# A hybrid encoder step on one core: the last chunk of the down projection splits its own late weight blocks, and its norms, copies and splits stand in another order

## The chip, the cores and the metric

The kernel runs on one core of a Trainium2 chip. The metric is the device time of one execution in microseconds (us). Three runs of the kernel before gave 1445.07, 1445.33 and 1449.37 us; their median is 1445.33 us.

## The reference, cut to what matters

One layer of an encoder works on 1024 prompt rows and 64 sample rows of width 1024, in float32. Three groups of heads mix the rows, a layer norm follows, and then the part that this change touches:

```python
def sq_relu_mlp(x, w_up, w_down):
    h = jnp.square(jax.nn.relu(jnp.einsum('btd,df->btf', x, w_up)))
    return jnp.einsum('btf,fd->btd', h, w_down)
...
        xp = layer_norm(ALPHA * xp + sq_relu_mlp(xp, w_up[l], w_down[l]), ln2_g[l], ln2_b[l])
```

`w_up` is 1024 x 4096 and `w_down` 4096 x 1024. The layer norm takes mean and variance over the 1024 values of a row and then multiplies by `ln2_g` and adds `ln2_b`.

## The kernel before, in words

TensorE (PE) multiplies float32 as three passes over a high and a low part in a rounded format. Every operand is **split** once (line 1182 is ACT's copy to the high part, line 97 the subtraction that makes the low part, on DVE or POOL). The split of h is a helper of its own, `h_split` (lines 1396, 1400, 1401): ACT copies a half to its high part, ACT copies that into a bank of PSUM (tile `st`, banks `o` and `tr` in turn), DVE subtracts.

The stages are: input projection, attention, output projection and first norm (to about 690 us), up projection (PE, line 1242, to about 1060 us), and **down**, from there to the end. h lies in DRAM, already transposed and combined.

**Down** runs over 8 chunks c of 512 rows of `w_down`. A chunk has two steps g = 2c and 2c + 1, each for half of the token tiles, and a step has two chains (class `Down`), one for tiles i and i + 4. A chain is seven products (`DOWN`), a Winograd form of a 2 x 2 block product; a product is 6 matmuls of 128 x 512. Products n = 0, 2, 4, 6 add up in one bank A, n = 1 goes into a bank B that ACT has filled beforehand (`preload`, line 1558), n = 3 and 5 into a bank D. Between two products into the same bank the bank must be read: after n = 0 by ACT (tile `p`, line 1587), after the others by DVE (line 1537, or 1580 where the sum of a row for the norm is taken along). So product n = 2 waits for the read of n = 0, n = 4 for that of n = 2, n = 5 for that of n = 3. Products 0 to 3 use h's first array (loaded into `awa`), 4 to 6 its second (`hr`, split by `h_split(g, 1, x)`).

The weights of chunk c + 1 are made during chunk c, one part q in each step. `wd_load` brings a raw part (512 KB twice) into the one buffer `rd`. Seven blocks are split from it (`wd_split`, k = 0 to 6): k = 0, 1, 2 from the raw blocks, then POOL overwrites them with differences (`wd_sums`, line 1371, four subtractions, called sum 0 to sum 3 here), and k = 3 to 6 are split from those: k = 4 needs sum 0, k = 5 sum 1, k = 3 sum 2, k = 6 sum 3. Sum 1 must also wait until DVE has split raw block 1 for the sample rows (tile `b`, one buffer, so its ACT copy waits for the previous chunk's sample products). The next part can be loaded only when all of this has read `rd`. The product order needs k = 0, 1, 3, 4, 5, 2, 6; k = 1, 2 are also read by `sample` (16 matmuls, lines 1614 and 1616).

**What sets the order.** In the loop over chunks a planner orders the instructions of every engine by its own estimate of time, so that a small edit can move instructions anywhere in the loop. The last chunk (c = 7, steps 14 and 15, four chains) stands in `in_order()`: on each engine its instructions keep the order of the source. `do(k, n)` is product n of chain k with the read of its bank. Between the products stand the layer norm of finished tiles: `neg_mean` (DVE), `squares` (ACT with a running sum, then POOL's `scale`, lines 1638 and 1639), `shift` (POOL), `normalize` (ACT, line 1663), `times` and `plus` (POOL, lines 1667 and 1671, and the store), or for the last tiles `on_dve` (lines 1679 and 1681) with copies of `ln2_g` and `ln2_b` in PSUM that `put_gb` makes (line 1731). ACT, DVE and POOL work their instructions off in order, so a waiting instruction holds back all behind it.

Of the kernel before, what the change touches and what calls it, by code (L numbers as in the profile page):

```python
# [12 lines left out]
F32 = mybir.dt.float32  # L13
# [43 lines left out]
def _build(nc, tc, a, es):  # L57
# [20 lines left out]
    def bcast(row, n=P):  # L78
        return row.broadcast_to([n, row.shape[-1]])
# [1279 lines left out]
    def wd_split(c, q, n, eng):  # L1359
        w = wset[c % 2][q]  # L1360
        b, src = ((0, 0), (1, 2), (2, 3), (5, 3), (3, 0), (4, 1), (6, 2))[n]
        split(w[:, 0, b], w[:, 1, b], raws[c, q][:, src], eng)
# [27 lines left out]
    def h_split(g, which, x, only=None):  # L1390

        for q in range(2):
            t = h_tile(g, which, x)
            o = 3 if which else 4
            raw = hraw[which, q][:, :, x * P:(x + 1) * P]
            nc.scalar.activation(t[:, 0, q], raw, AF.Copy)
            tag = only or ("o", "tr")[n_stage[0] % 2]
            n_stage[0] += 1
            st = ps.tile([P, 4, P], F32, name=f"st{n_stage[0]}", tag=tag, bufs=1)[:, 0:o]
            nc.scalar.activation(st, t[:, 0, q].bitcast(F32), AF.Copy)  # L1400
            nc.vector.tensor_tensor(t[:, 1, q], raw, st, op=ALU.subtract)  # L1401
# [104 lines left out]
    with ExitStack() as p3:  # L1506
# [100 lines left out]
        def sample(c):  # L1607
            for half in range(2):
                z = ps.tile([P, 512], F32, name=f"ds{c}_{half}", tag="s" if c < NC - 1 else ("s", "pt")[half], bufs=2)
                for q in range(2):  # L1610
                    for f in range(2):

                        w = b12[q] if f == 0 and half else wset[c % 2][q][:, :, f + half]
                        nc.tensor.matmul(z, hs[:, q, f].rearrange("p h c -> p (h c)"), w[:, 0],
                                         start=(q == 0 and f == 0), stop=False, skip_group_check=True)
                        nc.tensor.matmul(z[0:TS], hs[:, q, f, 0], w[:, 1], start=False, stop=(q == 1 and f == 1),
                                         skip_group_check=True)
                add(c == 0, acc[NB, half], z)
# [26 lines left out]
        def squares(t):  # L1645
            st = norm(t)

            nc.scalar.activation(awa[:, 0], accf[t], AF.Square, bias=st[:, 12:13], accum_out=st[:, 13:14])
            scale(t, P, 1.0 / D)
# [11 lines left out]
        def normalize(t, n=P, c0=0):  # L1661
            y, st = accf[t][0:n, c0:D], norm(t)[0:n]
            nc.scalar.activation(y, y, AF.Identity, bias=st[:, 15:16], scale=st[:, 14:15])

        def times(t, n=P, c0=0):
            y = accf[t][0:n, c0:D]
            nc.gpsimd.tensor_tensor(y, y, g2[0:n, c0:D], op=ALU.mult)

        def plus(t, n=P, c0=0):
            y = accf[t][0:n, c0:D]  # L1670
            nc.gpsimd.tensor_tensor(y, y, b2[0:n, c0:D], op=ALU.add)
            nc.sync.dma_start(out_rows(t)[:, c0:D], y)
# [11 lines left out]
        for c in range(NC - 1):  # L1684
            for part in range(2):
                g = 2 * c + part
                wd_load(c + 1, part)
                ch = [Down(g, x) for x in range(2)]
                for q in range(2):
                    h_load(g + 1, 0, q)  # L1690
                for n in range(7):
                    for d in ch:
                        d.product(n)
                    for d in ch:
                        d.evac(n)
                    if n < 2:
                        h_split(g, 1, n)
                    if n == 1:
                        for q in range(2):
                            h_load(g + 1, 1, q)  # L1700
                    if n == 3 and part == 0:
                        sample(c)
                        hs_load(c + 1)
                    if n in (2, 4):
                        h_split(g + 1, 0, n // 2 - 1)
                    if n == 1:
                        for k in range(3):
                            wd_split(c + 1, part, k, nc.gpsimd)
                    if n == 3:
                        wd_b12(c + 1, part, nc.vector)  # L1710
                        wd_sums(c + 1, part, nc.gpsimd)
                    if n == 4:
                        for k in range(3, 7):
                            wd_split(c + 1, part, k, nc.vector if k in (4, 5) else nc.gpsimd)


        c = NC - 1
        gb2 = lp.tile([P, 2, D], F32, name="gb2", tag="wr")
        g2, b2 = gb2[:, 0], gb2[:, 1]
        nc.sync.dma_start(g2, bcast(a["ln2_g"]))  # L1720
        nc.sync.dma_start(b2, bcast(a["ln2_b"]))
        fixed = {b: ps.tile([P, 512], F32, name=f"last{b}", tag=tag, bufs=2) for b, tag in (("B", "s"), ("D", "pt"))}
        gbp = []
        ch = [Down(2 * c + k // 2, k % 2, fixed, norm) for k in range(4)]
# [3 lines left out]
        def put_gb():  # L1728
            for q, (src, tag) in enumerate(((g2, "o"), (g2, "tr"), (b2, "s"), (b2, "pt"))):
                gbp.append(ps.tile([P, 512], F32, name=f"gbp{q}", tag=tag, bufs=1 if q < 2 else 2))  # L1730
                nc.scalar.activation(gbp[q], src[:, q % 2 * 512:q % 2 * 512 + 512], AF.Copy)

        def do(k, n):
            ch[k].product(n)
            ch[k].evac(n)
# [8 lines left out]
        with in_order():  # L1744
            ch[0].preload()
            do(0, 0)
            h_split(g, 1, 0)
            do(0, 1)
            sample(c)
            do(0, 2)  # L1750
            h_split(g, 1, 1)
            for q in range(2):
                h_load(g + 1, 1, q)
            do(0, 3)
            fold(0)
            fold(1)
            h_split(g + 1, 0, 0)
            do(0, 4)
            moments(NB, 0, TS)
            moments(NB, 1, TS)  # L1760
            scale(NB, TS)
            shift(NB, TS, -1.0)
            ch[1].preload()
            do(0, 5)
            neg_mean(0)
            do(1, 0)
            h_split(g + 1, 0, 1)
            do(0, 6)
            neg_mean(4)
            normalize(NB, TS)  # L1770
            times(NB, TS)
            squares(0)
            shift(0)
            do(1, 1)
            plus(NB, TS)
            squares(4)
            shift(4)
            normalize(0)
            times(0)
            plus(0)  # L1780
            do(1, 2)
            h_split(g + 1, 1, 0)
            do(1, 3)
            h_split(g + 1, 1, 1)
            ch[2].preload()
            do(1, 4)
            do(1, 5)
            neg_mean(1)
            do(2, 0)
            put_gb()  # L1790
            normalize(4)
            times(4)
            do(1, 6)
            neg_mean(5)
            squares(1)
            shift(1)
            plus(4)
            do(2, 1)
            squares(5)
            normalize(1)  # L1800
            times(1)
            do(2, 2)
            on_dve(5, 0, 0)
            ch[3].preload()
            do(2, 3)
            on_dve(5, 1, 0)
            do(2, 4)
            on_dve(5, 0, 1)
            do(2, 5)
            neg_mean(2)  # L1810
            on_dve(5, 1, 1)
            squares(2)
            shift(2)
            plus(1)
            do(3, 0)
            normalize(2, c0=512)
            do(2, 6)
            neg_mean(6)
            squares(6)
            times(2, c0=512)  # L1820
            plus(2, c0=512)
            do(3, 1)
            on_dve(2, 0, 0)
            on_dve(2, 0, 1)
            do(3, 2)
            on_dve(6, 0, 0)
            do(3, 3)
            on_dve(6, 0, 1)
            do(3, 4)
            on_dve(6, 1, 0)  # L1830
            do(3, 5)
            neg_mean(3)
            squares(3)
            on_dve(6, 1, 1)
            do(3, 6)
            neg_mean(7)
            squares(7)
            for i in range(2):
                for step in range(2):
                    on_dve(3, i, step)  # L1840
            shift(7)
            normalize(7, c0=768)
            times(7, c0=768)
            plus(7, c0=768)
            for c0, c1 in ((0, 512), (512, 768)):
                for step in range(2):
                    on_dve(7, c0 // 512, step, c1)
# [23 lines left out]
```

## Time and profile before

| | |
|---|---|
| time of the profiled execution | 1445.71 us |
| its span, first to last instruction | 1444.0 us |
| instructions | 24224 |
| busy: PE / DVE / ACT / POOL | 93% / 70% / 50% / 42% of the span |
| PE, 1120 to 1249 us (three chunks of down) | busy throughout |
| PE, 1400 to 1425 us | 19.41 of 25 us, granted clock 0.86 |
| PE, 1425 to 1445 us | 8.42 of 20 us |

The rows of a timeline give start, duration, engine, line, operation, output and inputs, a count, and in brackets the time that the engine stood idle before it and what released it. A wait put down to one engine can hide another that had to be waited for as well. Matmuls overlap: back to back, one of 128 x 512 starts every 0.232 us (six in 1.39 us) though its row shows 0.39.

### The profile page before, as it was taken

The numbers are of one execution on the slowest core, as the hardware profiler recorded it, in microseconds if no ns is written. First come the engines' busy times: TensorE is split into PE (matmuls) and PEld (weight loads), VectorE is DVE, ScalarE is ACT, GpSimd is POOL, SyncE is SP. The second block draws the span as 40 slices with busy tenths as digits, with TensorE's granted clock in tenths as the row PEclk, the third lists the DMA queues.
The fourth block names the chain that finished last, engine by engine and source line by source line (L and its number), as shares of the span: only waits on it lengthen the run. The fifth ranks groups of instructions, "written<-read, shape, count | busy, mean of one in ns | idle before, by whom it ended". The sixth has DMA issues, their size and how long they took to land.

```text
span 1444.0 us, 24224 instructions
## 1 busy us (share of the span) xinstructions
PE 1337.6 (93%) x8827; PEld 1212.3 (84%) x8827; DVE 1009.8 (70%) x1802; ACT 720.3 (50%) x1561; POOL 610.6 (42%) x660
## 2 busy tenths in 40 slices
PE   7899999999999988989779999999959999999976
PEld 6899999998988986867779999999947787777755
DVE  3567565767885699786736877776677766777766
ACT  3366565656564674243323323222345666766664
POOL 2222323266564537564222222222245464655565
PEclk9999999999999999999989999999979999999998
DMA  7324232322213435331124434443484424334333
GB/s 212 80 75 111 62 106 72 78 55 65 64 34 83 131 98 154 125 101 42 54 86 163 165 116 160 148 136 129 161 281 163 164 95 150 136 127 150 113 106 117
DMA packets 146207, 168.59 MB, mean 117 GB/s; under 512 B 27036, under 2 KB 112348, under 8 KB 146088
## 3 DMA queue, kind: packets, MB, share of 16 engines
q1 hardware_dynamic: 146088, 167.04, 36.7%
q8 instruction: 70, 1.15, 0.3%
q14 instruction: 49, 0.40, 0.1%
HBM read 109.00 MB, written 51.71 MB: 111 GB/s over the span
## 4 chain that ended last, share of the span: by engine, by line
PE 58%; DVE 12%; POOL 9%; DMA 8%; ACT 6%; issue 6%; SPq 1%; DVEq 0%; POOLq 0%; ACTq 0%
PE zA L1242 9%; PE zD L1242 6%; PE kvfox L337 5%; PE kvsb L337 5%; PE A L1570 4%; PE zB L1242 3%; PE zC L1242 3%; POOL rd L1371 3%; POOL wd L97 3%; PE mx L232 3%; DMA rd<-w_down 2%; PE qfox L478 2%; PE D L1570 2%; PE Sfox L536 2%; PE qsb L478 2%
## 5 line engine op out<-in xcount | busy, mean ns | idle before, releaser
L97 POOL TENSOR_TENSOR wa<-wr,wa 128x512 fp32r<-128x512 f32 x45 | 68.7, 1554 | 230.2 <-ACT wa L1182 230.2
L97 POOL TENSOR_TENSOR wd<-rd,wd 128x512 fp32r<-128x512 f32 x80 | 109.4, 1382 | 87.5 <-ACT wd L1182 82.0
L232 PE MATMUL mx<-xT,oTb 128*128 128x512 f32 (+1 forms) x416 | 106.3, 407 | 3.0 <-ACT oTb L191 2.0
L1182 ACT ACTIVATE wd<-rd 128x512 fp32r<-128x512 f32 x112 | 68.3, 625 | 75.1 <-DMA rd<-w_down 30.7
L1242 PE MATMUL zA<-xo,ws 128*128 128x288 f32 (+1 forms) x720 | 96.7, 289 | 2.5 <-ACT sn L1251 2.5
L1242 PE MATMUL zD<-xo,ws 128*128 128x288 f32 (+1 forms) x720 | 98.3, 291 | 0.0
L1251 ACT ACTIVATE sn<-zA 128x288 f32<-128x288 f32 (+1 forms) x96 | 37.6, 393 | 119.8 <-PE zA L1242 106.4
L232 PEld LDWEIGHTS mx<-xT,oTb 128*128 128x128 f32 (+1 forms) x416 | 77.2, 191 | 22.6 <-ACT oTb L191 3.0
L1242 PEld LDWEIGHTS zA<-xo,ws 128*128 128x128 f32 x720 | 93.4, 189 | 3.0 <-ACT sn L1251 2.9
L1242 PEld LDWEIGHTS zD<-xo,ws 128*128 128x128 f32 x720 | 94.8, 191 | 0.2
L337 PE MATMUL kvfox<-wkvfox,xT 128*128 128x256 f32 (+3 forms) x624 | 91.6, 296 | 3.1 <-DVE fx L440 2.0
L522 POOL TENSOR_TENSOR sgsb<-sgsb,snsb 128x127 f32<-128x127 f32 (+7 forms) x48 | 58.8, 1227 | 78.5 <-DVE snsb L520 67.6
L1371 POOL TENSOR_TENSOR rd<-rd 128x512 f32<-128x512 f32 x56 | 81.1, 1448 | 22.7 <-DVE b L97 20.3
L337 PE MATMUL kvsb<-wkvsb,xT 128*128 128x256 f32 (+1 forms) x624 | 88.2, 287 | 0.0
L337 PEld LDWEIGHTS kvfox<-wkvfox,xT 128*128 128x128 f32 (+1 forms) x624 | 82.8, 196 | 4.7 <-DVE fx L440 2.2
L1570 PE MATMUL A<-wd,wd 128*128 128x512 f32 x312 | 84.9, 401 | 2.0 <-ACT p L1587 0.7
L520 DVE TENSOR_TENSOR_SCAN snsb<-snsb,one 128x128 f32<-128x128 f32 (+7 forms) x48 | 72.1, 1506 | 13.2 <-ACT snsb L519 12.6
L337 PEld LDWEIGHTS kvsb<-wkvsb,xT 128*128 128x128 f32 (+1 forms) x624 | 79.7, 188 | 0.2
L1570 PE MATMUL A<-wd,h4a 128*128 128x512 f32 x240 | 67.1, 402 | 9.9 <-POOL wd L97 4.7
L1570 PEld LDWEIGHTS A<-wd,wd 128*128 128x128 f32 x312 | 58.8, 191 | 19.2 <-DVE acc L1537 2.9
L1570 PEld LDWEIGHTS A<-wd,h4a 128*128 128x128 f32 x240 | 44.8, 190 | 23.6 <-POOL wd L97 6.5
L1401 DVE TENSOR_TENSOR wd<-hr,st 128x384 fp32r<-128x384 f32 x64 | 34.7, 550 | 39.3 <-ACT st L1400 39.2
(511 smaller groups left out, 3745.6 us busy)
## 6 DMA issues: line engine op xcount, KB each, us to landing
rd<-w_down SPq DMA_DIRECT2D x32, 512.0 KB, 4.5
awa<-h_dr SPq DMA_DIRECT2D x32, 512.0 KB, 4.5
wr<-w_up SPq DMA_DIRECT2D x15, 1024.0 KB, 5.5
h_dr<-hh SPq DMA_DIRECT2D x30, 512.0 KB, 3.2
hr<-h_dr SPq DMA_DIRECT2D x32, 384.0 KB, 3.1
h_dr<-hh SPq DMA_DIRECT2D x30, 384.0 KB, 3.2
raw<-w_in SPq DMA_DIRECT2D x44, 256.0 KB, 3.4
xr<-x_prompt SPq DMA_DIRECT2D x8, 512.0 KB, 6.2
```

The lines of the kernel that those rows point to most:

```text
L97: eng.tensor_tensor(out, src, hi.bitcast(F32), op=ALU.subtract)
L232: nc.tensor.matmul(acc[0:m], oT[:, k, hx, 0:m], wo[k // 4][hw][:, k % 4, cs], start=(i == 0), stop=(i == len(seq) - 1))
L337: nc.tensor.matmul(acc[0:n, c0:c0 + n1 - n0], xT[k // 4][:, k % 4, c:c + n], wt[:, k, hw, n0:n1], start=(i == 0), stop=(i == len(seq) - 1))
L478: nc.tensor.matmul(acc[:, 0:w], wq[:, k, hw, :], xT[k // 4][:, k % 4, c:c + w], start=(i == 0), stop=(i == len(seq) - 1))
L520: nc.vector.tensor_tensor_scan(g[:, 0:n][:, ::-1], g[:, 0:n][:, ::-1], one.broadcast_to([P, n]), 1.0, op0=ALU.mult, op1=ALU.bypass)
L522: nc.gpsimd.tensor_tensor(s[:, 0:n - 1], s[:, 0:n - 1], g[:, 1:n], op=ALU.mult)
L1182: nc.scalar.activation(hi, raw, AF.Copy)
L1242: nc.tensor.matmul(z, w[:, hw, k], xop(s, bo, hx)[:, k, :], start=(new and k == 0 and j == 0), stop=(k == 3 and j == 2), skip_group_check= ...
L1251: nc.scalar.activation(sn[:, (0, None, 1, None, 2)[i], 0:n], z, AF.Copy)
L1371: eng.tensor_tensor(r[:, o], r[:, x], r[:, y], op=ALU.subtract)
L1401: nc.vector.tensor_tensor(t[:, 1, q], raw, st, op=ALU.subtract)
L1570: nc.tensor.matmul(z, h[:, hx, q, o], wset[self.c % 2][q][:, hw, wb], start=((n in (0, 3) or n == 1 and self.c == 0) and q == 0 and j == 0 ...
```

## The change

In the loop, the low parts of k = 3 to 6 go to DVE, POOL, DVE, POOL instead of POOL, DVE, DVE, POOL; and in step 13 (the last of the loop, g = 13) these four splits are not issued any more. They stand in the last chunk instead, behind the products n = 0 and n = 1 of its first chain and behind `sample`, with low parts on POOL, DVE, DVE, POOL. The load of `ln2_g` and `ln2_b`, which goes into the same buffer as `rd`, moves behind them. Further on, the second splits of h for the third and fourth chain, the preload of the third chain, `put_gb`, and the norm of tile 4 change places:

```diff
                     if n == 4:
-                        for k in range(3, 7):
-                            wd_split(c + 1, part, k, nc.vector if k in (4, 5) else nc.gpsimd)
+
+                        for k in range(3, 7) if g < NP - 3 else ():
+                            wd_split(c + 1, part, k, (nc.gpsimd, nc.vector)[k % 2])
...
-        gb2 = lp.tile([P, 2, D], F32, name="gb2", tag="wr")
-        g2, b2 = gb2[:, 0], gb2[:, 1]
-        nc.sync.dma_start(g2, bcast(a["ln2_g"]))
-        nc.sync.dma_start(b2, bcast(a["ln2_b"]))
...
             do(0, 0)
+            wd_split(c, 1, 3, nc.gpsimd)
             h_split(g, 1, 0)
             do(0, 1)
+            wd_split(c, 1, 4, nc.vector)
             sample(c)
+            wd_split(c, 1, 5, nc.vector)
+            wd_split(c, 1, 6, nc.gpsimd)
+            gb2 = lp.tile([P, 2, D], F32, name="gb2", tag="wr")
+            g2, b2 = gb2[:, 0], gb2[:, 1]
+            nc.sync.dma_start(g2, bcast(a["ln2_g"]))
+            nc.sync.dma_start(b2, bcast(a["ln2_b"]))
             do(0, 2)
...
             do(1, 2)
-            h_split(g + 1, 1, 0)
+            ch[2].preload()
             do(1, 3)
-            h_split(g + 1, 1, 1)
-            ch[2].preload()
+            normalize(4)
+            times(4)
             do(1, 4)
+            plus(4)
             do(1, 5)
             neg_mean(1)
             do(2, 0)
-            put_gb()
-            normalize(4)
-            times(4)
+            h_split(g + 1, 1, 0)
             do(1, 6)
             neg_mean(5)
             squares(1)
             shift(1)
-            plus(4)
             do(2, 1)
+            h_split(g + 1, 1, 1)
+            put_gb()
             squares(5)
             normalize(1)
             times(1)
...
             on_dve(5, 1, 1)
+            do(3, 0)
             squares(2)
             shift(2)
             plus(1)
-            do(3, 0)
             normalize(2, c0=512)
```

No instruction is added or dropped. Down to the first chunk of down every engine has the same order as before; from there on the planner orders the loop anew.

## The prediction

> **What bounds the kernel now.** I read PE's timeline from 1040 us on, then ACT's, DVE's and POOL's over the last 100 us, then the granted clock in small windows. From 1120 to 1249 us PE is busy throughout, so whatever the planner reorders there can gain nothing; it can only lose. PE waits at the edge to the last chunk and once inside it:
>
> ```profile
> 1373.60 0.50 PE L1570 MATMUL A<-wd,h4a 128*128 128x512 f32 x1 [0.33 <-ACT wd L1182]
> 1374.95 0.73 PE L1570 MATMUL A<-wd,h4a 128*128 128x512 f32 x2 [0.84 <-POOL wd L97]
> 1376.10 0.96 PE L1570 MATMUL A<-wd,wd 128*128 128x512 f32 x3 [0.41 <-DVE acc L1537]
> ...
> 1382.05 1.66 PE L1570 MATMUL lastB<-wd,h4a 128*128 128x512 f32 x6 [1.13 <-ACT lastB L1558]
> ...
> 1407.07 2.92 PE L1570 MATMUL lastD<-wd,wd 128*128 128x512 f32 x6 [4.90 <-DVE acc L1537]
> 1409.79 4.16 PE L1570 MATMUL A<-wd,wd 128*128 128x512 f32 x12
> ```
>
> The first four waits are the edge: part 1 of chunk 7's weights comes late. The fifth is inside chunk 7, and the matmuls behind it are slow: the windows (length, then busy time of PE, PEld, DVE, ACT, POOL, then the clock) show why.
>
> ```profile
> 1402.00:1407.00 5.00, 0.17 (x1) 0.00 (x0) 1.69 (x4) 4.23 (x8) 4.67 (x7) 0.86 0.19 40
> 1407.00:1410.00 3.00, 2.93 (x7) 2.35 (x8) 1.64 (x5) 1.25 (x3) 2.92 (x2) 0.50 0.10 21
> 1410.00:1413.00 3.00, 3.00 (x9) 2.34 (x9) 0.91 (x3) 0.41 (x1) 0.89 (x1) 0.59 0.43 173
> ```
>
> 18 matmuls take 6.72 us from 1407.07 to 1413.79 where 18 x 0.232 would be 4.18: the idle stretch costs 4.9 + 2.5 = 7.4 us.
>
> **The edge.** POOL and ACT tell why part 1 is late:
>
> ```profile
> 1361.80 1.30 POOL L1371 TENSOR_TENSOR rd<-rd 128x512 f32<-128x512 f32 x1 [9.84 <-DVE b L97]
> ...
> 1366.87 2.56 POOL L97 TENSOR_TENSOR wd<-rd,wd 128x512 fp32r<-128x512 f32 x2
> ```
> ```profile
> 1380.88 0.63 ACT L1182 ACTIVATE wd<-rd 128x512 fp32r<-128x512 f32 x1 [3.63 <-POOL rd L1371]
> 1381.42 0.58 ACT L1558 ACTIVATE lastB<-awa 128x512 f32<-128x512 f32 x1
> ```
>
> In step 12 POOL idles 9.84 us until DVE has split `b` (ACT's copy at 1360.32), then does three sums, the sample's two and k = 3, 6; at 1369.43 the buffer is free, the load goes out at 1369.46 and the copy starts at 1372.92. Now, by the new orders:
>
> - k = 4 is POOL's (1.28 us) and lies in the 9.84 us of idleness; one low part, not two, follows the sums. 1.28 us earlier.
> - ACT's copy of `b` stood behind two copies of `hr` and an `st` (1359.07 to 1360.32); now it comes right behind the copies of `awa`. Those wait for loads that waited for DVE's reads of `awa`; DVE no longer has the split of k = 4 (1.16) and a bank read (0.60) ahead of these, of which I count 1.3, as `st` comes at 1351.65. So `b` at 1357.8; `sample` is 6 matmuls earlier in PE's order and done by 1355.9.
> - Sums from 1359.1: 1.30 + 0.89 + 3.01 to 1364.3; ACT's last copy for k = 6 stands behind that of k = 3 and a `p`, so k = 6 ends at 1366.2; DVE's k = 3 (1.5 us beside POOL) by 1365.1. Free 3.2 us earlier, the load's copy at 1369.7.
>
> PE comes to part 1's first matmul at 1371.75, so its three waits for it go. Next late is DVE's low part of `b` (copy 1370.3 to 1370.8, 1.34 us) with three instructions of 0.60 behind it: the read that the next product waits for ends at 1373.9, PE comes at 1373.85. The preload of B (1381.42) stood behind a copy that waited for sum 1; now it stands ahead of it. With no wait left the 30 matmuls from 1371.05 end at 1378.1 and lastB starts there, not at 1382.05: 3.9 us. Behind it the moved splits: k = 3's low part (POOL) ends at 1381.6 and is needed at 1383.3, k = 4 (DVE, behind B's read) at 1383.9 for 1384.7, k = 5 at 1385.7 for 1386.1; their reads of the bank push n = 4 by 0.3 and n = 5 by 0.2, and the copies for `fold` (1390.04 before) come at 1386.85. So what hangs on ACT and DVE in chain 0 is **3.2 us** earlier; POOL's `times(NB)` follows. The load of `ln2_g` moves behind k = 5 (1385.8, before 1386.44); it is needed 10 us later. SP's second `hr` load now waits behind the weights' load; it is read 12 us later. Bounds: 1.3 (only POOL's one instruction counts) and 4.0.
>
> **The tail.** I give it in the old clock and take the 3.2 us off at the end. The wait of 4.90 is this: ACT's `normalize(0)` (1402.68) waits for POOL's `times(NB)` and `scale(0)`; h's splits stand behind it on ACT, DVE's subtraction behind them, and behind that the read of D:
>
> ```profile
> 1402.68 1.24 ACT L1663 ACTIVATE awa<-awa,lstb 128x1024 f32<-128x1024 f32 x1 [1.30 <-POOL lstb L1659]
> 1403.83 0.51 ACT L1396 ACTIVATE wd<-hr 128x384 fp32r<-128x384 f32 x1
> ```
>
> With the splits gone, DVE reads D at once and PE goes on at 1402.1. Now what comes late:
>
> - ACT: `normalize(0)` to 1403.9, preload to 1404.45; `normalize(4)` waits for POOL's `plus(NB)` (1402.60 to 1404.94) and `scale(4)`, `shift(4)` to 1406.11: 1406.15 to 1407.4. Then `p` of chain 2 to 1407.9 (PE is there at 1407.7), two copies and two `st` (0.97 a pair, as at 1403.92 to 1405.82) to 1409.85, `squares(1)` (1.15) to 1411.0, the other four to 1412.95.
> - DVE's subtractions for these end at 1413.5 and stand ahead of the read of A after (2, 2): 1414.15. PE has finished (2, 3) at 1410.8 and starts (2, 4) at 1414.2: **a new wait of 3.4 us**. Before, (2, 4) started at 1417.99.
> - `put_gb` now follows (2.15 us, to 1415.1), then `squares(5)` to 1416.3, which `on_dve(5)` must wait for since it overwrites what is squared; the read of D after (2, 3) stands behind that, 1417.65. (2, 5) starts at 1417.7, having waited 2.1 us; before at 1420.24.
> - POOL: `times(0)`, `plus(0)`, `times(4)`, `plus(4)` (2.37 to 2.40 each) fill it from 1406.1 to 1415.7, `scale(5)` ends at 1417.6; DVE needs it at 1419.0. `normalize(1)` ends at 1417.9, the preload of chain 3 at 1418.4, needed at 1421.9.
> - (3, 0) now precedes `squares(2)` on ACT, so its `p` is ready before (3, 2) and the wait of 0.72 at 1426.83 goes. PE's last product starts at 1428.95 (1432.57 before). DVE is then the bound: its last eight `on_dve` start at 1431.75, not 1435.15. **3.4 us** earlier; behind them nothing changes.
>
> **Sum.** 3.2 + 3.4 = 6.6 us off the profiled execution's 1445.71: **1439.1 us** (the median of the runs, 1445.33, is 0.4 below that execution; against it the gain is 6.2 us or 0.43%).
>
> **The loop.** Over chunks 0 to 6 I count nothing. For step 10 by the new orders: the two preloads of B are done at 1319.65 and 1323.2, PE needs them at 1320.7 and 1323.75; `p` at 1322.0 for 1322.35. Bounds: 1.5 gained (the waits of 1.04 at 1276.02, 0.34 and 0.15 later go) and the price of the third rival.
>
> **Rivals.**
>
> 1. *The clock falls in the new wait.* For: the 4.90 us of idleness above were followed by 0.50. Against: 3.4 us is shorter, and the 2.45 us before 1051.25 left the clock at 1.00 in the window of 1051 to 1054. At half speed (2, 4) takes 2.8 us, which the wait for (2, 5) hides; (2, 5) and part of (3, 0) would lose 2 us: 1441.1. The Trainium skill ("TensorE: Matmul & The Clock Gate", "What's actually happening") says that the clock is halved after at least one idle window of about 3.4 us and that the window runs freely; by it a gap of 3.4 us seldom covers a whole one, and the sum stays. The trace agrees on the half (0.50); where its windows lie it can't show.
> 2. *The wait only moves.* If the copies, `squares(1)` and `put_gb` cost what the old wait did, (2, 4) and (2, 5) start 3.4 us later than I say and the edge alone is left: 1442.5. For: the eight copies stand in front of (2, 4) now. Likewise if the load comes only 1.3 us sooner: 1441.0.
> 3. *The loop gets slower: the case on the other side.* In the loop ACT now has the preloads of B behind the copies for k = 5 and 6 and `p` behind k = 3, all waiting for POOL's sums. My slack is 0.35 to 1.05 us. A sum takes 1.25 to 1.63 us; if three take the upper value more often than I reckon, the preload is late. At 1.0 us in each of 13 parts PE loses 13 us: 1452.1, slower. It decides from 0.5 us a part, where the gain is gone. For: any wait there is a loss, PE having no slack. Against: the waits of this kind in the old loop came to 1.5 us in all.
>
> **How the numbers follow.** About 0.3% (4.3 us) can be told from no change. My forecast, between 1436 and 1441: 54%. The clock or the moved wait, 1441 to 1443: 26%. The loop: 20%, half of it only eating the gain (1443 to 1449), half slower than that. So faster 0.55, within 0.34, slower 0.11. The range goes from 1436.0 (4.0 at the edge, 3.4 in the tail and 1.5 in the loop give 1436.8; 0.8 more should the new waits be shorter) to 1446.5, which leaves out most of the slower loop.
>
> **What would show it.** Right: lastB starts straight behind g = 13's last matmul; the load of part 1 is issued about 3 us before its place now; (1, 5) follows (1, 4) without a wait; the longest wait of PE in chunk 7 is ahead of (2, 4), 3 to 4 us, released by DVE, with the clock at 1.00 behind it; then 2 us ahead of (2, 5). Wrong: waits of PE for ACT's `B` or `p` spread over the loop, a clock of 0.5 behind the new wait, or a last `on_dve` group that starts no earlier relative to PE's last product.

## The result, and the profile after

The changed kernel takes **1438.82 us**, the median of six runs (1437.36 to 1442.09). Beside them the kernel before has 1446.62 us, also of six. The ratio is 0.9948, with a 95% interval of 0.9932 to 0.9964: 5.2 to 9.8 us less. The profiled execution of the changed kernel took 1441.04 us, 4.67 less than that of before.

PE's timeline of the profile after, at the edge and then inside the last chunk (start, duration, operation, count, and in brackets the wait and its releaser):

```profile
1376.57 0.84 PE L1570 MATMUL A<-wd 128*128 128x512 f32 x3
1377.47 1.66 PE L1570 MATMUL lastB<-wd,h4a 128*128 128x512 f32 x6
...
1404.89 1.56 PE L1570 MATMUL lastD<-wd,wd 128*128 128x512 f32 x6
1409.64 2.90 PE L1570 MATMUL A<-wd,wd 128*128 128x512 f32 x6 [3.18 <-DVE acc L1537]
1413.17 2.93 PE L1570 MATMUL lastD<-wd,wd 128*128 128x512 f32 x6 [0.63 <-DVE acc L1537]
1415.89 4.44 PE L1570 MATMUL A<-wd,wd 128*128 128x512 f32 x12
```

The four waits of the edge are gone: lastB starts straight behind the matmuls ahead of it, 4.58 us earlier than before. The wait of 4.90 is gone too, and in its place one of 3.18 stands ahead of (2,4), product 4 of chain 2. The windows of the same execution (length, busy time of PE, PEld, DVE, ACT, POOL, then the clock) show what followed it:

```profile
1406.00:1409.00 3.00, 0.45 (x2) 0.01 (x1) 2.47 (x8) 2.83 (x8) 2.92 (x3) 0.98 0.44 175
1409.00:1412.00 3.00, 2.36 (x6) 1.84 (x6) 0.72 (x2) 2.73 (x5) 2.83 (x3) 0.50 0.00 0
1412.00:1415.00 3.00, 2.37 (x6) 1.49 (x5) 3.00 (x6) 1.73 (x2) 2.31 (x5) 0.50 0.44 178
1415.00:1418.00 3.00, 3.00 (x8) 2.31 (x7) 1.61 (x5) 0.00 (x0) 1.05 (x1) 0.50 0.23 87
1418.00:1421.00 3.00, 3.00 (x12) 2.42 (x11) 0.63 (x2) 1.73 (x3) 0.41 (x2) 0.81 0.23 87
```

The clock is at 0.50 for some 10 us, longer than before (from 1405.6 to 1412.5 there). So the last eight `on_dve` start at 1430.22, 4.93 us earlier than before, hardly more than lastB: in this execution the new tail is worth 0.35 us.

The edge itself, on POOL, ACT and SP's queue of the profile after:

```profile
1356.21 0.77 POOL L97 TENSOR_TENSOR hs<-acc,hs 128x128 fp32r<-128x128 f32 x1 [5.71 <-ACT hs L1182]
1356.94 1.30 POOL L1371 TENSOR_TENSOR rd<-rd 128x512 f32<-128x512 f32 x1
...
1362.69 1.30 POOL L97 TENSOR_TENSOR wd<-rd,wd 128x512 fp32r<-128x512 f32 x1 [1.07 <-ACT wd L1182]
```
```profile
1364.02 0.81 SPq L1357 DMA_DIRECT2D rd<-w_down  x2
```

POOL's idle time of 9.84 ahead of sum 1 is 5.71 now, one low part instead of two follows the sums, and the load of part 1 goes out at 1364.02 instead of 1369.46. On ACT the copies of h are gone from behind `normalize(0)`; a preload follows it at once:

```profile
1398.07 1.25 ACT L1663 ACTIVATE awa<-awa,lstb 128x1024 f32<-128x1024 f32 x1 [1.29 <-POOL lstb L1659]
1399.22 0.58 ACT L1558 ACTIVATE lastB<-acc 128x512 f32<-128x512 f32 x1
```

To see where the time went, I divided each profiled execution at four marks: the four matmuls into A that wait for POOL's low part (1072.44 before), the first matmul `ds<-b` of chunk 0 (1091.13), the first into lastB (1382.05), and the last eight `on_dve` (1435.15). Between the first two lies the **head**, between the next two **loop and edge**, then the **tail**. Loop and edge hold the same 1220 matmuls in all kernels; in most of it one starts every 0.231 us, which makes 281.8 us of work for PE.

| execution | shares in the loop | head starts | head | loop and edge | tail | clock behind the tail's first wait |
|---|---|---|---|---|---|---|
| before | old | 1072.44 | 18.69 | 290.92 | 53.10 | 0.50 |
| e2_tail | old | 1069.87 | 18.59 | 294.78 | 52.57 | 0.50 |
| e4_moved | old | 1065.85 | 19.69 | 295.51 | 52.08 | 0.50 |
| e8_late | old up to step 11 | 1069.62 | 22.34 | 292.02 | 52.66 | 0.50 |
| after | new | 1072.34 | 21.30 | 283.83 | 52.75 | 0.50 |
| after_again | new | 1072.59 | 20.65 | 283.63 | 50.10 | 1.00 |
| e1_edge | new | 1069.44 | 19.86 | 283.64 | 52.94 | 0.50 |
| e3_swap | new | 1069.86 | 19.89 | 284.52 | 52.52 | 0.50 |
| e5_fill | new | 1073.80 | 20.81 | 282.60 | 50.10 | 1.00 |
| e6_early | new | 1073.76 | 20.73 | 282.95 | 48.02 | 1.00 |
| e6_again | new | 1071.87 | 20.78 | 284.98 | 48.04 | 1.00 |
| e7_alt | other alternation | 1070.33 | 19.81 | 283.38 | 53.01 | 0.50 |
| e10_both | other alternation | 1073.13 | 18.81 | 286.27 | 48.03 | 1.00 |
| e9_first | old in step 0, then new | 1075.25 | 18.80 | 284.34 | 48.00 | 1.00 |

Before against after: the head starts 0.10 earlier and takes 2.61 longer, loop and edge take 7.09 less, the tail 0.35 less, and what lies behind it 0.23 more: -4.70, the difference of the spans. The start of the head differs by some 9 us from execution to execution; nothing ahead of it is changed in any kernel. Three heads hold one more wait, for DVE's read L1535 late in the head: e4_moved 1.13, e7_alt 1.26, e8_late 2.53.

### The profile page after: what moved, and what is told of

Same layout as the page of the kernel before. It is cut to its first block, busy times and chain, and to the rows that moved or that the text cites. A ratio compares the mean times of both kernels' runs of the same rounds, so it can differ in the third digit from the quotient of the medians.

```text
span 1439.3 us, 24229 instructions
## 1 busy us (share of the span) xinstructions
PE 1340.2 (93%) x8827; PEld 1217.8 (85%) x8827; DVE 1010.3 (70%) x1802; ACT 720.3 (50%) x1561; POOL 610.5 (42%) x660
## 4 chain that ended last, share of the span: by engine, by line
PE 67%; DVE 9%; DMA 7%; ACT 7%; POOL 4%; issue 4%; SPq 1%; DVEq 0%; ACTq 0%; POOLq 0%
PE zA L1242 9%; PE mx L232 7%; PE zD L1242 6%; PE A L1570 6%; PE kvsb L337 5%; PE kvfox L337 4%; PE zB L1242 3%; PE zC L1242 3%; PE D L1570 3%; PE qsb L478 2%; DMA rd<-w_down 2%; PE qfox L478 2%; POOL wd L97 2%; PE Sfox L536 2%; PE B L1570 1%
## 5 line engine op out<-in xcount | busy, mean ns | idle before, releaser
L1438 ACT ACTIVATE ws<-wr 128x1024 fp32r<-128x1024 f32 x30 | 31.2, 1057 | 58.4 <-DVE wr L1192 58.4
```

The lines of the kernel that those rows point to most:

```text
L1438: nc.scalar.activation(ws[:, 0, q], raw[:, q], AF.Copy)
```

## The experiments

Twelve runs, in three groups of four; those of one group share a chip and the runs of the kernel before (medians 1445.62, 1448.15 and 1448.33 us).

**e1_edge: the loop's and the edge's part of the change, the old tail.** Against the changed kernel:

```diff
             do(1, 2)
-            ch[2].preload()
+            h_split(g + 1, 1, 0)
             do(1, 3)
-            normalize(4)
-            times(4)
+            h_split(g + 1, 1, 1)
+            ch[2].preload()
             do(1, 4)
-            plus(4)
...
```

> The loop's new shares and the late splits inside chunk 7, with the old order from product (1, 2) on. I read two stretches: L, from the second sample group of chunk 0 (b row) to lastB's first start (290.92 us before, 283.83 after), and T, from there to the end of the last on_dve (58.55 before, 58.20 after). Theory: loop and edge are a gain of their own, L as after (283 to 285), T as before (58 to 59, with the wait of 4.9 and the clock of 0.5 behind it), so about 7 us faster than before. Rival (the wait only moves): what is won at the edge is waited for again in chunk 7, T 3 us or more longer, 0 to 4 us faster.

Measured: 1436.70 us (1435.21 to 1441.16), ratio 0.9945 (0.992 to 0.997); loop and edge 283.64, tail 52.94. None of the edge's four waits is left, the wait of 4.9 inside the chunk is back. So loop and edge hold the whole gain that the medians show.

**e2_tail: the kernel before with the new tail alone.** Against before:

```diff
             do(1, 2)
-            h_split(g + 1, 1, 0)
+            ch[2].preload()
             do(1, 3)
-            h_split(g + 1, 1, 1)
-            ch[2].preload()
+            normalize(4)
+            times(4)
             do(1, 4)
+            plus(4)
...
```

> The old loop and the old edge, with the new order from product (1, 2) on. Theory: L as before (290 to 291); the wait of 4.9 goes, a new one of 3.2 ahead of (2, 4) comes, T 55 to 56 if the clock stays at 1.00 behind it, 58 if it falls to 0.5: 3 us faster or the same as before, by the clock. Rival (the tail is the whole gain): 5 us or more faster.

Measured: 1446.60 us (1439.96 to 1451.80), ratio 1.0003 (0.9982 to 1.0024). The wait ahead of (2,4) is 3.20, the clock fell behind it, the tail takes 52.57. No gain that can be measured.

**e3_swap: the other shares in all 14 steps, nothing else.**

```diff
                         for k in range(3, 7):
-                            wd_split(c + 1, part, k, nc.vector if k in (4, 5) else nc.gpsimd)
+                            wd_split(c + 1, part, k, (nc.gpsimd, nc.vector)[k % 2])
```

> Only the shares of the low parts in the loop as after, in all 14 steps; the splits of k = 3 to 6 of the last part stay in step 13, and chunk 7 keeps its old order. Theory: k = 4 lies in POOL's idle time and the load of part 1 goes out 3 to 5 us sooner than before, so the loop and the first three waits of the edge gain, 5 to 6 us, L 285 to 286; lastB still waits for ACT, whose copies for the sums stand ahead of its preload (about 1 us). Rival (the late splits in chunk 7 are the gain): L 289 or more, within 2 us of before.

Measured: 1439.04 us (1434.89 to 1442.28), ratio 0.9951 (0.9935 to 0.9966); loop and edge 284.52, within a microsecond of the whole change. At the edge a single wait of 1.34 for DVE's read is left. This one line makes the measurable gain by itself, though the title names only the last chunk's part of the change.

**e4_moved: only the late splits moved into the last chunk; old shares, old tail.**

```diff
-                        for k in range(3, 7):
+                        for k in range(3, 7) if g < NP - 3 else ():
...
             do(0, 0)
+            wd_split(c, 1, 3, nc.gpsimd)
...
+            wd_split(c, 1, 4, nc.vector)
```

> Only the last part's splits of k = 3 to 6 inside chunk 7; shares in the loop and the order from (1, 2) on as before. Theory: part 1's load is as late as before, the waits of 0.33, 0.84 and 0.41 at the edge stay, only lastB's preload comes sooner: L 289 to 290, 1 to 2 us faster. Rival (late splits are the gain): L 284 to 286, 5 to 7 us faster.

Measured: 1444.79 us (1442.27 to 1449.90), ratio 1.0004 (0.9986 to 1.0021); loop and edge 295.51, above both theories. The wait of 1.13 ahead of lastB is gone, but the three ahead of it stand (0.41, 0.84, 0.41), and the clock fell among them, from 1375.1 to 1378.5. The moved splits alone bring nothing.

**after_again: the changed kernel once more.**

> The changed kernel once more, beside the three others of this call. Theory (the gain is the loop's and the edge's, the tail's is lost to the granted clock): a median of 1437 to 1440 us, from the second sample group of chunk 0 to the first product into lastB 283 to 285 us (283.83 in the first profile), from there to the last eight on_dve 52.5 to 53 us if the clock falls again behind the new wait ahead of (2,4), 49.5 to 50 us if it does not. Rival (the head and the clock differ by chance from execution to execution): the head's products at 0.50 this time only until 1078, as in the profile before, and so a lastB some 2 to 3 us earlier.

Measured: 1437.36 us (1432.22 to 1444.21), ratio 0.9928 (0.9905 to 0.9952). The head was again at half clock up to 1087, and loop and edge took 283.63; but the tail took 50.10 instead of 52.75. Its windows:

```profile
1406.00:1409.00 3.00, 0.00 (x0) 0.00 (x0) 2.43 (x6) 2.83 (x7) 2.92 (x2) 1.00 0.43 175
1409.00:1412.00 3.00, 1.63 (x6) 1.05 (x6) 0.79 (x2) 2.33 (x5) 2.67 (x5) 1.00 0.17 72
1412.00:1415.00 3.00, 2.39 (x10) 1.99 (x11) 3.00 (x6) 1.58 (x2) 2.47 (x3) 1.00 0.25 105
```

The same program with the same wait (3.19) ahead of (2,4), and the clock did not fall. This is the tail as I forecast it: 3.00 us shorter than before's. The difference between the two executions, 2.65 us, is what the half clock costs.

**e5_fill: twelve more matmuls in the new wait.** They go into the bank that (3,0) uses later.

```diff
+        def fill(n):
+            ch[3].open("A")
+            for k in range(n):
+                nc.tensor.matmul(ch[3].bank["A"], h_tile(2 * c + 1, 0, 0)[:, 0, 0, 0], wset[c % 2][0][:, 0, 0],
+                                 start=(k == 0), stop=(k == n - 1), skip_group_check=True)
...
             do(2, 3)
+            fill(12)
```

> The changed kernel with twelve more matmuls of 128 x 512 behind product (2,3), into the bank that product (3,0) overwrites later, so that PE works in the new wait ahead of (2,4); their result is not used. Theory (the wait itself costs little at the end, the half clock behind it costs about 3 us): the wait is gone or under 0.5 us, the clock stays at 1.00 from 1406 to 1425, lastB to the last eight on_dve takes 49.5 to 50.5 us instead of 52.75, and the kernel is 2 to 3.5 us faster than the changed one. Rival (DVE and ACT's order sets the end, not the clock): clock at 1.00, but 52 us and more as before, no faster than the changed kernel.

Measured: 1438.16 us (1436.37 to 1439.21), ratio 0.9931 (0.9914 to 0.9949). The clock stays at 1.00 and the tail takes 50.10, as in after_again to the hundredth: (2,4) starts 32.21 us behind lastB in both, so the fill neither delays it nor brings it sooner. The gain of 2 to 3.5 us over the changed kernel did not show: its median beside it was 1437.36. Beside it the clock is known of one execution of the changed kernel only, and there it had not fallen; how often it falls isn't known. The spread was 2.8 us in five runs against 12 us in the changed kernel's six beside it. But in the first six runs of the changed kernel it was 4.7 us, so the clock is not shown to make the spread.

**e6_early: products (2,2) and (2,3) ahead of the last split of h.** Against the changed kernel:

```diff
             do(2, 1)
+            do(2, 2)
+            do(2, 3)
             h_split(g + 1, 1, 1)
+            ch[3].preload()
             put_gb()
             squares(5)
-            normalize(1)
-            times(1)
-            do(2, 2)
+            do(2, 4)
             on_dve(5, 0, 0)
-            ch[3].preload()
-            do(2, 3)
             on_dve(5, 1, 0)
-            do(2, 4)
-            on_dve(5, 0, 1)
             do(2, 5)
             neg_mean(2)
-            on_dve(5, 1, 1)
+            on_dve(5, 0, 1)
             do(3, 0)
+            normalize(1)
+            times(1)
+            on_dve(5, 1, 1)
             squares(2)
```

> The changed kernel with products (2,2) and (2,3) ahead of the fourth chain's last split of h, put_gb and the squares of tile 5 behind the preload of the fourth chain, and the on_dve of tile 5 and the norm of tile 1 later. Theory (the wait ahead of (2,4) stands because DVE reads the bank of (2,2) only behind the split's subtractions and on_dve): the wait ahead of (2,4) falls from 3.18 to under 1 us, the clock stays at 1.00, lastB to the last eight on_dve takes 48 to 50.5 us, and the kernel is 2 to 5 us faster than the changed one. Rival (the wait only moves: (3,0) or (3,4) waits for what was put off): some 3 us of wait elsewhere ahead of the fourth chain, the clock at 0.50 behind it, and no gain.

Measured: 1436.29 us (1433.18 to 1436.69), ratio 0.9917 (0.9899 to 0.9934). PE's timeline:

```profile
1408.03 1.63 PE L1570 MATMUL A<-wd,wd 128*128 128x512 f32 x6 [1.59 <-DVE acc L1537]
...
1419.55 1.65 PE L1570 MATMUL A<-wd,wd 128*128 128x512 f32 x6 [1.49 <-DVE acc L1537]
```

The wait ahead of (2,4) is halved, not under 1 us; 1.49 has moved ahead of (3,4), half of what the rival said. The clock stays at 1.00 and the tail takes 48.02, 2.1 less than the changed kernel's at full clock. By the medians the gain over the changed kernel (1.1 us) lies within the spread.

**e7_alt: the other alternation (POOL, DVE, POOL, DVE) in the kernel before.**

```diff
-                            wd_split(c + 1, part, k, nc.vector if k in (4, 5) else nc.gpsimd)
+                            wd_split(c + 1, part, k, (nc.vector, nc.gpsimd)[k % 2])
```

> The kernel before with the low parts of k = 3 to 6 on POOL, DVE, POOL, DVE in all 14 steps of the loop, the other alternation. Theory (the loop gains since DVE has no two of these splits in a row that hold back bank reads and h's subtractions): gains as e3_swap does, 1437 to 1441 us, from the second sample group to lastB 284 to 287 us. Rival (what counts is that k = 3, which the product order wants first, is on DVE, where it takes 0.7 to 1.5 us behind no sum, instead of behind three sums on POOL): no gain or a loss, 1444 to 1449 us, 290 us and more, with waits of products on the low part of k = 3 from POOL.

Measured: 1439.92 us (1436.93 to 1444.98), ratio 0.9959 (0.9941 to 0.9978); loop and edge 283.38. It gains like e3_swap, so it is not that k = 3 went to DVE. But the planner reorders the loop for any such edit (in the traces at least 355 of PE's 8827 matmuls stand in another place than in before here, 270 in e3_swap), and the time cannot tell the shares from the order that comes with them.

**e8_late: the new shares in the last two steps of the loop only.**

```diff
-                            wd_split(c + 1, part, k, nc.vector if k in (4, 5) else nc.gpsimd)
+                            wd_split(c + 1, part, k, nc.vector if k in ((3, 5) if g > 11 else (4, 5)) else nc.gpsimd)
```

> The kernel before, with the new shares only in the last two steps of the loop (g = 12 and 13), which split the last chunk's weights; everything else as before. Theory (the gain has two places, the loop's earlier chunks and the way into the last chunk, and each gains from its own shares): from the sample row that opens chunk 6 to the first product into lastB 28.7 to 30.5 us (32.4 before), the six chunks ahead of it 262 to 268 us as in the three kernels with the old shares, the head's wait ahead of (A, six matmuls, released by ACT's p) 1.5 us as before, and a median some 2 to 4 us under before. Rival (the way into the last chunk is late because the loop is late, so shares there alone change nothing): 32 us and more, and no gain.

Measured: 1448.00 us (1445.39 to 1454.71), ratio 1.0006 (0.9990 to 1.0023). My theory fell, the rival held: no gain. The two waits for W_down itself are gone, that for DVE's read is left, but PE comes to lastB as late as ever:

```profile
1383.98 1.66 PE L1570 MATMUL lastB<-wd,h4a 128*128 128x512 f32 x6 [2.93 <-ACT lastB L1558]
```

The load of part 1 does follow that of part 0 sooner, after 24.91 us instead of 27.05. But the wait of 1.13 has become 2.93: ACT's preload starts only at 1383.32, after 1.74 us of idleness that a read of DVE (L1537) ended. Up to 1353 us every engine works in before's order here. In these runs the edge is won only together with the loop.

**e9_first: e6_early with the old shares in step 0.**

```diff
-                            wd_split(c + 1, part, k, (nc.gpsimd, nc.vector)[k % 2])
+                            wd_split(c + 1, part, k, nc.vector if k in ((3, 5) if g else (4, 5)) else nc.gpsimd)
```

> e6_early, with the old shares in step 0 of the loop alone, so that block k = 4 of chunk 1 goes to DVE again in the head of down. Theory (the new shares cost some 2 us in the head, since POOL makes that low part there while PE waits for DVE and POOL, and PE then takes up the next products at half clock): the wait ahead of the six matmuls into A that ACT's p releases falls from 3.30 to about 1.5 us, from the four matmuls into A behind POOL's low part to the second sample group 18.5 to 19 us instead of 20.7, and a median 1.5 to 2.5 us under e6_early. Rival (the head's clock is chance, and the loop's order takes up what the head loses): no gain over e6_early, or a longer loop (over 285 us from the second sample group to lastB).

Measured: **1433.50 us** (1430.05 to 1437.31), ratio 0.9895 (0.9872 to 0.9918), the best of all; e6_early's second run, beside it, has 1437.26. The wait is 1.55 and the head 18.80, both as the theory says. Its profiled execution is its slowest run (1437.31); its head started at 1075.25, 3.4 us later than e6_again's, which may be why. The gain of 3.8 us in the median is more than the 2 of the head; six runs each do not tell whether the rest is chance.

**e10_both: e6_early with the other alternation.**

```diff
-                            wd_split(c + 1, part, k, (nc.gpsimd, nc.vector)[k % 2])
+                            wd_split(c + 1, part, k, (nc.vector, nc.gpsimd)[k % 2])
```

> e6_early, with the low parts of k = 3 to 6 on POOL, DVE, POOL, DVE in all steps of the loop. Theory: the head as in e7_alt (wait 1.46 us there, 19.8 us to the second sample group), 283 to 284 us to lastB, 48 us from there to the last eight on_dve; a median 0.5 to 1.5 us under e6_early. Rival (the other order of the loop that comes with it gives the gain back): 284 to 288 us to lastB and no gain over e6_early.

Measured: 1435.79 us (1432.45 to 1437.70), ratio 0.9918 (0.9897 to 0.9939). The head takes 18.81, since k = 4 is DVE's here too, but loop and edge take 286.27, with waits of 0.27 to 0.57 in six places. In this execution most of the head's 2 us is given back, as the rival said; the median is 1.5 us under that of e6_again, as the theory said. The intervals overlap, so neither is shown.

**e6_again: e6_early beside these.**

> e6_early once more, on the chip of the three others. Theory (no wait of 3 us stands in its tail, so the clock stays at 1.00 there): 1434 to 1437 us, a spread of its times within 4 us (the changed kernel's is 12 us), and 48 us from lastB to the last eight on_dve. Rival (the clock may fall behind its waits of 1.5 us too): 50 us and more in the tail and times up to 1440 us.

Measured: 1437.26 us (1434.13 to 1438.73), ratio 0.9927 (0.9906 to 0.9948). Tail 48.04, clock at 1.00 behind both waits, as the theory says; the median and the spread of 4.6 us lie just outside what it gave.

## Why the prediction was right, and where it was right by luck

I forecast 1439.1 us; the median is 1438.82. The sign and the size are right, but the sum of 6.6 us was two terms, and four places moved. The baseline helped too: I took the sum off one execution of before (1445.71). By the medians of six runs the gain is 7.8 us, by the two profiled executions 4.67.

**The edge: right, and slightly too small.** I had 3.9 us at lastB and kept 3.2 of it in the last chunk. From the sample row that opens chunk 6 to lastB it took 32.44 us before and 28.73 after: 3.71. All of it is kept: behind lastB the old tail takes 52.94 in e1_edge and 53.10 before. The chain of reasons was right up to its size: ACT's copy of `b` comes at 1355.32, 5.0 us earlier, where I had 2.5. It needs shares and moved splits together: e3_swap leaves a wait of 1.34, e4_moved leaves three.

**The tail: the mechanism right, its gain mostly lost in the profiled execution.** (1,5) follows without a wait; the new waits stand where I put them, 3.18 ahead of (2,4) (I said 3.4) and, at full clock, 1.90 ahead of (2,5) in after_again (2.1). At full clock the tail gains 3.00 us, where I had 3.4. But **the first rival happened**, in this execution and in e2_tail: with the clock at 0.50 the gain is 0.35. I priced that at 2 us, it cost 2.65. My evidence against it, one gap of 2.45 us that left the clock alone, was too thin: the same 3.2 us let it fall in two executions of three. By the rule of the Trainium skill ("TensorE: Matmul & The Clock Gate", "What's actually happening"), cited beside it, the sum would have stayed; the runs show that a window need not be idle for the clock to fall (see the last section).

**The loop: this is the step that failed.** I wrote "Over chunks 0 to 6 I count nothing", with 1.5 us as the most to gain. Loop and edge went from 290.92 to 283.83, and less the edge's 3.71 that is 3.38 us in the loop. The third rival (a slower loop) had the wrong sign. I had read PE's busy time, which hides much. The windows of before, where the second number is PE's busy time and the count of matmuls stands behind it:

```profile
1200.00:1210.00 10.00, 10.00 (x42) 7.50 (x41) 5.80 (x9) 6.35 (x12) 9.39 (x7) 1.00 0.01 2
1270.00:1280.00 10.00, 8.85 (x38) 6.68 (x38) 6.64 (x10) 8.08 (x19) 7.86 (x7) 1.00 0.14 44
```

A full window holds 44 to 46, mostly 45, so "busy 10.00" with 42 is short by some 0.7 us. From 1120 to 1250 us before and after have 559 and 557 matmuls: there was nothing to gain there, as I said. But from 1250 to 1370 it is 505 against 519, and 14 x 0.232 = 3.2 us. One place of it can be followed. ACT and PE in chunk 5 before:

```profile
1272.71 0.63 ACT L1182 ACTIVATE wd<-rd 128x512 fp32r<-128x512 f32 x1 [1.92 <-POOL rd L1371]
1273.25 0.92 ACT L1396 ACTIVATE wd<-hr 128x384 fp32r<-128x384 f32 x2
```
```profile
1276.02 0.49 PE L1570 MATMUL D<-wd 128*128 128x512 f32 x1 [1.04 <-DVE wd L1401]
```

ACT waits 1.92 us for POOL's sum with the copies of h queued behind; DVE's subtraction for h comes late, and PE waits. After:

```profile
1272.27 0.51 ACT L1396 ACTIVATE wd<-hr 128x384 fp32r<-128x384 f32 x1
...
1273.24 0.51 ACT L1396 ACTIVATE wd<-hr 128x384 fp32r<-128x384 f32 x1
1274.31 0.63 ACT L1182 ACTIVATE wd<-rd 128x512 fp32r<-128x512 f32 x1 [0.56 <-POOL rd L1371]
```

Two copies of h stand ahead of the one that waits. The diff does not say that; the planner did it, given the new shares. The wait of 1.04 to 1.48 stands in all four kernels with the old shares and in none with the new. More telling is the table: with the old shares lastB comes at 1381.0 to 1384.0 whether the head is over at 1085.5 or at 1092.0, so something other than PE sets the pace; with the new ones it follows the head by 282.6 to 285.0, little more than the 281.8 of PE's own work. One step more can be read on SP's queue, from the load of part 1 of chunk 3 to that of chunk 7, before and then after:

```profile
1191.71 0.81 SPq L1357 DMA_DIRECT2D rd<-w_down  x2
...
1369.46 0.81 SPq L1357 DMA_DIRECT2D rd<-w_down  x2
```
```profile
1195.22 0.81 SPq L1357 DMA_DIRECT2D rd<-w_down  x2
...
1364.02 0.81 SPq L1357 DMA_DIRECT2D rd<-w_down  x2
```

A chunk takes 44.44 us of this round before and 42.20 after, where PE's 184 matmuls take 42.5. In the four kernels with the old shares it is 44.1 to 45.2, in the ten others 41.8 to 42.8. In before the round from chunk 3 to chunk 4 takes 45.06 us, and PE starts 191 matmuls in it, seven more than a chunk has: the weights fall behind PE before PE waits for long. Most of the difference lies between the two loads of a chunk, 25.8 to 28.0 us with the old shares from chunk 4 on and 23.6 to 25.0 with the new. Which wait stretches it in the old order, and whether shares or order cure it, stays open.

**The head: not in the sum at all.** I never looked at what the shares do in step 0, whose splits begin while DVE still works off the up projection. POOL and PE before:

```profile
1070.94 4.83 POOL L97 TENSOR_TENSOR wd<-rd,wd 128x512 fp32r<-128x512 f32 x3
```
```profile
1080.40 1.64 PE L1570 MATMUL A<-wd,h4a 128*128 128x512 f32 x6 [1.55 <-ACT p L1587]
```

And after:

```profile
1070.83 6.08 POOL L97 TENSOR_TENSOR wd<-rd,wd 128x512 fp32r<-128x512 f32 x4
```
```profile
1082.01 2.93 PE L1570 MATMUL A<-wd,h4a 128*128 128x512 f32 x6 [2.42 <-ACT p L1587]
```

POOL has four low parts where it had three (k = 4 of chunk 1 is the fourth), at a stage where PE waits for POOL and DVE anyway; PE's wait grows, and the six matmuls then run at half clock (2.93 against 1.64). The head costs 1.2 to 2.7 us more with the new shares than in before and e2_tail, and e9_first takes it back.

So the profiled gain is: edge 3.7, loop 3.4, tail 0.35, head -2.6, less 0.1 at the two ends. What I missed in the loop about made up for the head and the tail's clock. The forecast was right by its edge and by that balance, not by its tail.

## What to carry to other kernels

Count matmuls in a window, not PE's busy time: a stretch that is 100% busy can still be 7% short, and that is where an edit to another engine's load pays. When work changes engines in every step of a loop, look at the first step, where the stage before is still running, as well as the steady state; there may be a different answer for it (step 0 here). And a wait of some 3 us on PE is a lottery for the clock: put work there or split the wait in two (1.59 and 1.49 left the clock alone in four executions of four, though the last section shows a 1.48 that did not). That the spread of the times shrinks with it is not shown: e9_first has no such wait in its tail and a spread of 7.3 us.

## What the hardware showed unasked

The half clock lasts a whole number of windows of **3.41 us**, and the grid of windows is fixed for an execution: the low stretches measured in half-microsecond windows were 3.41 us (e4_moved three times, e8_late), 6.83 (before, e1_edge, e2_tail, e3_swap, e7_alt, e8_late), 10.24 (after) and 13.66 in all in after_again's head. In the execution after, the clock rose in the head at 1088.05 and fell in the tail at 1408.90, 94.0 windows of 3.413 us later; in before it is 1077.94 and 1405.62, 96.0 windows. So the trace does show where the windows lie, which the prediction said it could not. How the grid lies against the kernel differs between executions, so the same wait of 3.2 us can cost nothing or 2.65 us. The length agrees with the window of about 3.4 us in the Trainium skill ("TensorE: Matmul & The Clock Gate", "What's actually happening"). That it takes an idle window to fall does not agree: e4_moved fell behind a wait of 1.48 us.

```profile
1273.00:1275.00 2.00, 0.53 (x2) 0.10 (x1) 2.00 (x4) 2.00 (x6) 1.92 (x2) 1.00 0.11 33
1275.00:1276.00 1.00, 0.96 (x3) 0.49 (x3) 1.00 (x2) 1.00 (x3) 1.00 (x2) 1.00 0.00 0
1276.00:1277.00 1.00, 0.93 (x2) 0.83 (x3) 0.75 (x3) 1.00 (x3) 0.28 (x1) 0.55 0.00 0
```

The clock fell at 1276.10; in the 3.41 us ahead of that PE had been busy for about 1.8 us, with six matmuls, one of them in part. In after_again two windows with six matmuls each did not let it fall, so about six of the 14.7 that fit is where it turns. Over all fourteen executions, from 1070 to 1430 us and with shares of matmuls counted, the clock fell behind every full-clock window with up to 5.4 and behind none with 5.8 or more. At half clock 7.35 fit; windows with up to 6.1 did not bring the clock back, those with 6.3 or more did. In the execution after, the windows from 1408.90 and from 1412.32 held 5.7 and 6.0. The second of them has the short wait of 0.63 in it, and that is why this wait made the low stretch longer.
